# Moving the norms' sums to token partitions by small transfers, and making the last six tiles' sums in strips

## The chip, the cores and the metric

The kernel runs on one core of a Trainium2 chip. The core has TensorE (PE, the matmul engine, whose weight loads the profile lists apart as PEld), VectorE (DVE), ScalarE (ACT), GpSimd (POOL) and SyncE (SP), which here does nothing but issue transfers. Each engine runs its own instructions in order; semaphores make one wait for another. The metric is device time in microseconds (us) of one execution, the median of several.

## The reference

An encoder layer works on two sequences, a prompt of 256 tokens and a sample of 2,048, with a model width of 1,024, in float32:

```python
h = rms_norm(x, g_pre)
q, k, v, z_a, u_f, z_f = split(h @ w_in)            # six parts of width 512
y_a = neighbourhood_attention(q, k, v, rpb)         # 8 heads of 64, windows of 8 x 16 on a grid 64 wide
y_f = fourier_mix(u_f, w_fourier, b_fourier)        # 2-D FFT, real part, then a matrix and a bias
mixed = concat([rms_norm(y_a, g_na) * silu(z_a),
                rms_norm(y_f, g_f) * silu(z_f)])
out = mixed @ w_out
return x + rms_norm(out, g_post)
```

where `rms_norm(x, g) = x * rsqrt(mean(x * x) + 1e-6) * g` over the last axis. What matters here are the two norms in `mixed`: for each of the 2,304 tokens one factor from the mean square of 512 values of `y_a`, and one of `y_f`.

## The kernel before

The tokens are cut into 18 tiles of 128. Both halves of `mixed @ w_out` are made apart: for a tile, the product of the un-normed half with its part of `w_out` stands in PSUM with the tokens on the partitions, and its factor is applied on the way out, as one number for each partition. The factors stand in `invf` (Fourier half) and `inva` (attention half), tiles of 128 x 18, one column for each token tile. Values `y`, on the other hand, are kept with the channels on the partitions and the tokens along the free axis, and so are the sums of squares over the channels' blocks: `sqs` (Fourier) and `ysq` (attention), both 128 x 2,304. To get a factor, the 128 partitions of `sqs` or `ysq` have to be summed and the result, a row of tokens, be turned so that the tokens lie on partitions.

The part of the program around the change is written in a set order by hand: PE always, and from the last Fourier block on also ACT, DVE, POOL and SP run their instructions in the order in which the source issues them. It has two stages:

1. **The attention loop** (L1577), k from 2 to 36. There are 36 groups `G` (four pairs of heads, nine groups each). Step k makes the scores of group k (`scores`, L1184), its softmax (DVE L1206, ACT L1211, POOL L1218), and, for group k-1, the transposes of the weights in two halves (`transp`, L1508, into the PSUM tiles `ptb[0]` and `ptb[1]`, copied out as `pt` by ACT and DVE) and the product with the values (`pv`, L1524, into the PSUM tile of tag `c`, of which there is one). Between them stand 12 output matmuls of the Fourier half (`f_mm`, L1435, PSUM tile `po`), whose evacuation `f_evac` applies `invf`. `pv` also writes squares of `y_a` into `ysq` (ACT, and POOL from the second pair on). In steps 2 to 7 the last Fourier block's squares are made by ACT (L1634) and added into `sqs` by DVE (L1635), for the token ranges in the table `YSQ`; step 5 treats tokens 512 to 1,109, step 6 those to 1,707 and step 7 the rest. At the end of a step SP issues the loads of the next groups: `prep_v` (`v` and `za`, one step ahead) and `prep` (`ql`, three steps ahead). `split_q` on ACT takes `ql` up.
2. **The output loop** over the 18 tiles of the attention half (index j): `a_mm` (24 matmuls of 512 columns a tile), `a_evac` with `inva`, the last norm, and the residual.

The norms' factors are made like this. `norm_sums` multiplies the squares by a block of ones, 128 x 32, so that up to four token tiles land side by side as strips of 32 equal rows of `ptb[0]`; ACT copies them to the SBUF tile `nsb`, of which there is one. One step later `norm_turn` transposes `nsb` with PE into the PSUM tile `pn` (tag `c`), where each strip's first column holds the tokens of a tile on the partitions, and `rsq_ops` makes the factor: two ACT instructions (L1381 and L1382), one on DVE (L1383), and three more on DVE, which `run_later` issues somewhat later. The table `NT` tells in which step which tiles are turned: Fourier tiles in steps 4, 8, 10, 11, 12, attention tiles in 32, 34, 36, and the sums stand in the step before. The first two Fourier tiles are done by `f_norm`, and the last six attention tiles by `a_norm` at j=1: matmuls with a tile of `ysq` as weights and one column of ones, which put the tokens onto partitions at once.

The program has eight semaphores for transfers that SP uses in turn, and each transfer waits, before it is issued, until the eighth transfer before it has landed.

Of the kernel before, what the change touches and what calls it, by code (L numbers as in the profile page):

```python
# [10 lines left out]
F32 = mybir.dt.float32  # L11
# [157 lines left out]
def build(tc, A, O):  # L169
    nc = tc.nc  # L170
# [23 lines left out]
    ident = cst.tile([128, 128], F32, name="ident")  # L194
    ones = cst.tile([128, 1], F32, name="ones")
# [7 lines left out]
    invf = cst.tile([128, 18], F32, name="invf")  # L203
    inva = cst.tile([128, 18], F32, name="inva")
# [9 lines left out]
    ps = es.enter_context(tc.tile_pool(name="ps", bufs=3, space=PSUM))  # L214
# [503 lines left out]
    for c in range(3, 6):  # L718
# [7 lines left out]
        if c == 4:  # L726
# [33 lines left out]
    for b in range(16):  # L760
# [13 lines left out]
        if 2 <= b < 8:  # L774
            x, y = divmod(b, 2)
# [349 lines left out]
    def prep(g):  # L1125
        pr, ts = g["pr"], g["ts"]
        g["qh"] = jl.tile([128, 256], F32R, tag="qh", name="qh", bufs=4)
        g["ql"] = jl.tile([128, 256], F32R, tag="ql", name="ql", bufs=4)
        if g["R"] is None:
            q = qD[pr, :, ts].rearrange("p (b x) -> p b x", b=2)  # L1130
        else:
            sg, x = divmod(g["R"], 2)
            t0 = TP + 1024 * sg + 512 * g["hc"]
            q = qD[pr, :, t0:t0 + 512].rearrange("p (b x) -> p b x", b=2)[:, :, 128 * x:128 * x + 128]
        nc.sync.dma_start(g["ql"].bitcast(F32).rearrange("p (b x) -> p b x", b=2), q)
# [258 lines left out]
    def run_later():  # L1394
        while later:
            later.pop(0)()
# [79 lines left out]

    nsb = []

    def norm_sums(sq, ts):
        n = 32 * len(ts)  # L1480
        for x, t in enumerate(ts):
            nc.tensor.matmul(ptb[0][32 * x:32 * x + 32, :128], ones32, sq[:, t * 128:t * 128 + 128], start=True, stop=True)
        o = sm.tile([128, 128], F32, name="nsb", bufs=1)[:n]
        nc.scalar.copy(o, ptb[0][:n, :128])  # L1484
        nsb.append(o)

    def norm_turn(dst, ts):
        o = nsb.pop()
        n = 32 * len(ts)
        p = ps.tile([128, 128], F32, tag="c", name="pn", bufs=1)[:, :n]  # L1490
        nc.tensor.transpose(p, o, ident[:n, :n])
        ts = slice(ts[0], ts[-1] + 1)
        rsq_ops(dst[:, ts], p[:, ::32], ts.stop - ts.start, 1.0 / 512)

    def a_norm(ds):
        p = ps.tile([128, 128], F32, tag="c", name="pna", bufs=1)
        for j, d in enumerate(ds):
            nc.tensor.matmul(p[:, j:j + 1], ysq[:, d["t"] * 128:d["t"] * 128 + 128], ones, start=True, stop=True)
        n = len(ds)
        rsq_ops(inva[:, ds[0]["i"]:ds[0]["i"] + n], p[:, :n], n, 1.0 / 512)  # L1500

    def transp(g, b):
        ch = g["ch"][b]
# [13 lines left out]
    def pv(g):  # L1517
# [28 lines left out]
        if R is None or hc:  # L1546
# [1 line left out]

    WO = []

    NT = {4: range(2, 4), 8: range(4, 8), 10: range(8, 12), 11: range(12, 16), 12: range(16, 18),
          32: range(4), 34: range(4, 8), 36: range(8, 12)}

    YSQ = {2: [(Y2, 256, 512), (Y2, 512, 1024)], 3: [(Y, 256, 512), (Y2, 1024, 1664)], 4: [(Y2, 1664, 2304)],
           5: [(Y, 512, 1110)], 6: [(Y, 1110, 1708)], 7: [(Y, 1708, 2304)]}
# [17 lines left out]
    prep_v(G[2])  # L1573
    prep(G[4])
    ones32 = sm.tile([128, 32], F32, name="ones32", bufs=1)
    nc.vector.memset(ones32, 1.0)
    for k in range(2, len(G) + 1):  # L1577
        pr, i = divmod(k, 9)
        g, f = G[k] if k < len(G) else None, G[k - 1] if k else None
        if pr < 3:  # L1580
            if i == 3:
                KK[pr + 1] = load_k(pr + 1)
                for x in range(2):
                    fetch_k(KK[pr + 1], pr + 1, x)
            if i == 7:
                load_t(pr + 1, 0)
        if 0 < pr < 4 and i == 0:
            load_t(pr, 1)
        if pr < 4 and i == 3:
            load_t(pr, 2)  # L1590
        if k == 9:
            nc.sync.dma_start(gpb, pbc(A["gpost"]))
        if k == 23:
            wp = pt.enter_context(tc.tile_pool(name="wp", bufs=1, side="right"))
            WO.extend(wp.tile([128, 4, D], F32R, name="w0%d" % x) for x in range(2))
        if 24 <= k < 32:
            y = k - 24
            nc.sync.dma_start(WO[y % 2][:, y // 2].bitcast(F32), woD[0, y % 2, y // 2])
        x = k // 2 + 1
        if g:  # L1600
            scores(g)
            if 2 < k < 34 and k % 2 == 0:
                ys_mul(ftiles[x])
                if x + 1 < 18:
                    ys_load(ftiles[x + 1])
            bias_max(g, 0, 0)
            exps(g, 0, 0)
            bias_max(g, 0, 1)
            bias_max(g, 1, 0)
        if f:  # L1610
            transp(f, 0)
        if g:
            exps(g, 0, 1)
            bias_max(g, 1, 1)
            exps(g, 1, 0)
            f_mm(k, range(6))
            soft(g, 0)
            exps(g, 1, 1)
        else:
            a_mm(atiles[0], 0, range(6))  # L1620
        if k in NT:
            norm_turn(invf if k < 32 else inva, NT[k])
        if f:
            transp(f, 1)
        if g:
            if k + 1 < len(G):
                split_q(G[k + 1])
            soft(g, 1)
            if k == 2:
                ys_mul(ftiles[x])  # L1630
                ys_load(ftiles[x + 1])
        run_later()
        for v, x0, x1 in YSQ.get(k, []):
            nc.scalar.activation(v[:, x0:x1], v[:, x0:x1], AF.Square)  # L1634
            V.tensor_tensor(out=sqs[:, x0:x1], in0=sqs[:, x0:x1], in1=v[:, x0:x1], op=ALU.add)  # L1635
# [12 lines left out]
        if g:  # L1648
            f_evac(k)
        if f:  # L1650
            pv(f)
        if k + 1 in NT:
            norm_sums(sqs if k < 31 else ysq, NT[k + 1])
        if k == 12:
            pq_.close()
        if k + 1 < len(G):
            prep_v(G[k + 1])
        if k + 3 < len(G):
            prep(G[k + 3])
        if k == 28:  # L1660
            xk = [kp.tile([128, T], F32, tag=x, name="xk") for x in ("kh", "kl")]
        if 32 <= k < 36:
            x, d = k - 32, atiles[k - 32]
            d["xt"] = xk[x // 2][:, x % 2 * D:x % 2 * D + D]
            nc.sync.dma_start(d["xt"], A["xn"][d["t"] * 128:d["t"] * 128 + 128, :])
        if k == 32:
            ys_load(atiles[0])
        if k in (34, 35):
            ys_load(atiles[k - 33])
            of_load(atiles[k - 34])  # L1670
        if k == 36:
            ys_split(atiles[1])
# [65 lines left out]
    for j, d in enumerate(atiles):  # L1738
        if j + 3 < 18:
            ys_load(atiles[j + 3])  # L1740
        for x in range(2, 5) if j == 0 else (j + 4,):
            if x < 18:
                of_load(atiles[x])
                if x > 3:
                    xt_load(atiles[x])
        if j:
            a_mm(d, 0)
        if j == 1:
            a_norm(atiles[12:])
            run_later()  # L1750
        a_evac(d, 0)
        if j + 2 < 18:
            y_hi(atiles[j + 2])
        if j == 0:
            for n in range(2):
                nc.scalar.copy(ptb[n], gpb[:, n * 512:n * 512 + 512])
        if j == 17:
            last_tile(d, atiles[16])
            break
        if j:  # L1760
            factor(atiles[j - 1])
# [24 lines left out]
```

## Time and profile before

| | |
|---|---|
| Median of three runs | 970.5 us (969.4 to 972.34) |
| The profiled execution | 971.28 us, span of its instructions 969.5 us |
| Granted TensorE clock | 0.998 |
| PE, PEld | 959.5 us (99%), 800.4 us (83%) |
| DVE, ACT, POOL | 705.4 us (73%), 496.1 us (51%), 429.8 us (44%) |
| DMA | 279.37 MB in 146,382 packets, 288 GB/s in the mean |

A row of the timeline gives the start in us from the span's start, the duration in us, the engine, the source line, the operation with what it writes and reads, the shape and a count, since like neighbours are merged; in brackets stands how long the engine was idle before it, and what ended that. `SPq` rows are the issuing of transfers. For PE a shape such as 128*32 128x512 gives the rows and columns of the array that are used, and the moving operand. A row of a line's or tile's view gives the smallest, middle and largest duration in ns, then the first and last start. A row of the waits gives the total in us, how often, and the longest. Float32 matmuls with a full-precision operand appear as two instructions each (12 for the six of `a_norm`).

### The profile page before, as it was taken

Reading aid. Unit: us, or ns where it says so; the run is one execution under the profiler, and the core shown is the slowest. Engines: PE = TensorE matmul, PEld = TensorE weight load, DVE = VectorE, ACT = ScalarE, POOL = GpSimd, SP = SyncE. Lnnn points to the kernel's source line nnn. Section 1 sums busy time; section 2 is a strip of 40 time slices with the busy share of each in tenths; the row PEclk is TensorE's granted clock in tenths of the full one; section 3 lists DMA queues with packets and bytes.
Section 4 is the critical chain, followed back from the end, with each engine's and each line's share of the span. In section 5 each row is a group of like instructions: output and inputs, shape, how many; then the busy total and the mean of one; then the engine's idle time right before and its main releaser. Section 6 shows DMA issues by size and latency. Waiting matters only on the chain.

```text
span 969.5 us, 17019 instructions
## 1 busy us (share of the span) xinstructions
PE 959.5 (99%) x5745; PEld 800.4 (83%) x5745; DVE 705.4 (73%) x1306; ACT 496.1 (51%) x1078; POOL 429.8 (44%) x400
## 2 busy tenths in 40 slices
PE   9999999999999999999999999999999999999997
PEld 7889988888888888888888879878787888878886
DVE  6758988687886777797877345776765656649997
ACT  6835676423334533233344256677666676744443
POOL 3100002464751202665655033567677686524544
PEclk9999999999999999999999999999999999999999
DMA  9898796557748997599889898689877998979993
GB/s 334 309 380 316 256 346 245 199 198 261 294 186 353 343 413 258 198 364 344 308 297 333 294 324 328 190 272 297 264 227 249 278 302 283 293 253 324 344 338 133
DMA packets 146382, 279.37 MB, mean 288 GB/s; under 512 B 13730, under 2 KB 84216, under 8 KB 142904
## 3 DMA queue, kind: packets, MB, share of 16 engines
q1 hardware_dynamic: 145864, 277.89, 81.9%
q8 instruction: 46, 0.75, 0.3%
q10 hardware_dynamic: 432, 0.39, 0.1%
q14 instruction: 40, 0.33, 0.1%
HBM read 183.85 MB, written 101.52 MB: 294 GB/s over the span
## 4 chain that ended last, share of the span: by engine, by line
PE 94%; DMA 1%; DVE 1%; SPq 1%; issue 1%; ACT 1%; POOL 1%; DVEq 0%; ACTq 0%; POOLq 0%
PE po L1435 20%; PE mm L165 18%; PE mm L164 17%; PE mm L166 17%; PE pv L1524 5%; PE ptb L1508 5%; PE s L1184 4%; PE pab L1024 2%; DMA ut<-uN 1%; PE py L164 1%; PE py L166 1%; PE py L165 1%; SPq L367 1%; DMA gpre<-gpre 0%; PE ppq L1062 0%
## 5 line engine op out<-in xcount | busy, mean ns | idle before, releaser
L164 PE MATMUL mm<-xh,wa 128*128 128x512 f32 x448 | 174.4, 389 | 0.0
L165 PE MATMUL mm<-xl,wa 128*128 128x512 f32 x448 | 174.3, 389 | 0.0
L166 PE MATMUL mm<-xh,wa 128*128 128x512 f32 x448 | 174.3, 389 | 0.0
L536 POOL TENSOR_TENSOR ws<-wr 128x512 f32<-128x512 f32 x16 | 23.5, 1468 | 228.0 <-DMA wr<-wz 224.0
L1218 POOL TENSOR_SCALAR w<-w,m 128x465 f32<-128x465 f32 (+9 forms) x136 | 85.2, 639 | 44.1 <-DVE m L1215 34.1
L164 PEld LDWEIGHTS mm<-xh,wa 128*128 128x128 f32 x448 | 84.1, 188 | 17.7
L166 PEld LDWEIGHTS mm<-xh,wa 128*128 128x128 f32 x448 | 84.1, 188 | 17.4
L165 PEld LDWEIGHTS mm<-xl,wa 128*128 128x128 f32 x448 | 84.1, 188 | 17.4
L1435 PE MATMUL po<-wo,yh 128*128 128x512 f32 x272 | 90.5, 414 | 0.0
L551 DVE TENSOR_TENSOR wa<-wr,wa 128x512 fp32r<-128x512 f32 x60 | 69.3, 1162 | 27.2 <-ACT wa L550 27.0
L1435 PE MATMUL po<-w,yh 128*128 128x512 f32 x280 | 86.7, 391 | 0.0
L1211 ACT ACTIVATE w<-w,m 128x465 f32<-128x465 f32 (+9 forms) x136 | 78.3, 579 | 15.5 <-DVE m L1206 15.5
L1206 DVE CUSTOM_DVE_ANT_1 w<-s,tb 128x465 f32<-128x465 f32 (+8 forms) x124 | 61.2, 531 | 9.7 <-PE s L1184 9.2
L165 PE MATMUL mm<-vl,xh 128*128 128x512 f32 x168 | 65.6, 390 | 0.2 <-DVE vl L482 0.2
L166 PE MATMUL mm<-vh,xl 128*128 128x512 f32 x168 | 65.4, 389 | 0.0
L164 PE MATMUL mm<-vh,xh 128*128 128x512 f32 x168 | 65.4, 389 | 0.0
L589 POOL TENSOR_TENSOR mt<-mt,rmask 128x880 f32<-128x880 f32 (+2 forms) x24 | 50.8, 2131 | 32.1 <-DVE mt L585 19.8
L877 DVE TENSOR_TENSOR f<-u,mm 128x512 f32<-128x512 f32 x64 | 43.5, 680 | 29.2 <-PE mm L166 24.3
L1435 PEld LDWEIGHTS po<-w,yh 128*128 128x128 f32 x280 | 52.3, 188 | 10.9 <-issue 0.2
L1508 PE MATMUL ptb<-ident,w 128*120 128x128 f32 (+8 forms) x422 | 58.9, 277 | 1.0 <-ACT nsb L1484 0.9
L550 ACT CAST wa<-wr 128x512 fp32r<-128x512 f32 x60 | 36.4, 617 | 44.8 <-PE mm L166 19.3
L1508 PEld LDWEIGHTS ptb<-ident,w 128*120 128x120 f32 (+8 forms) x422 | 47.2, 140 | 13.8 <-issue 8.0
(263 smaller groups left out, 2391.8 us busy)
## 6 DMA issues: line engine op xcount, KB each, us to landing
wr<-wz SPq DMA_DIRECT2D x48, 512.0 KB
vl<-sD SPq DMA_DIRECT2D x20, 512.0 KB
xm<-xm SPq DMA_DIRECT2D x9, 1024.0 KB
oD<-ofs SPq DMA_DIRECT2D x18, 512.0 KB
of<-oD SPq DMA_DIRECT2D x18, 512.0 KB
yr<-yD SPq DMA_DIRECT2D x34, 256.0 KB
zD<-f SPq DMA_DIRECT2D x16, 512.0 KB
woD<-wo SPq DMA_DIRECT2D x16, 512.0 KB
```

The source lines that it names most:

```text
L164: nc.tensor.matmul(out, lh, rh, start=first, stop=False)
L165: nc.tensor.matmul(out, lh, rl, start=False, stop=False)
L166: nc.tensor.matmul(out, ll, rh, start=False, stop=last)
L551: nc.vector.tensor_tensor(out=o[:, 1], in0=src, in1=o[:, 0].bitcast(F32), op=ALU.subtract)
L589: nc.gpsimd.tensor_tensor(out=o, in0=i, in1=rmask[:, m0:m0 + n].unsqueeze(2).to_broadcast([128, n, 80]), op=ALU.add)
L877: nc.vector.tensor_tensor(out=dst(f, b), in0=src(uu[u]), in1=src(p), op=op)
L1206: nc.vector.tensor_tensor_reduce(out=rows(g["w"][b][:, h, :n], w), in0=rows(g["s"][2 * b + h][:, :nr * sw(w)], sw(w))[:, :, :w], in1=tv, s ...
L1211: nc.scalar.activation(w, w, AF.Exp, bias=m[:, h:h + 1], scale=-1.0, accum_out=m[:, 2 + h:3 + h])
L1218: nc.gpsimd.tensor_scalar(w, w, m[:, 4 + h:5 + h], 1.0, ALU.mult, ALU.mult)
L1435: nc.tensor.matmul(p, (d["l"] if x == 2 else d["h"])[:, c], w(n, int(x == 1), c), start=j == 0, stop=j == 11)
L1508: nc.tensor.transpose(ptb[h][:nk, j * 128:j * 128 + 128], g["w"][b][:, h, c0:c0 + nk], ident)
L1524: nc.tensor.matmul(p[hs, b], g["v"][:nk, v, hs], g["pt"][b][:nk, h, j * 128:j * 128 + 128], start=j == 0, stop=j == len(ch) - 1)
```

## The change

The turn by PE stays for the first group of Fourier tiles (step 4) only. For all others, `norm_move` sends, from `nsb`, the first row of each strip (128 floats on one partition) by a transfer of its own to one column of a new SBUF tile `ssum` (128 x 18, one float on each of 128 partitions). SP issues these at the end of the step in which the sums are made, behind `prep_v` and `prep`. `norm_root` then makes the factors from `ssum`, two and a half steps after the sums. So the sums of Fourier tiles 4 to 15 move to steps 5, 7, 9 (from 7, 9, 10); the attention tiles' sums stay in 31, 33, 35, and their roots come in 34, 36 and, for tiles 8 to 11, at j=1 of the output loop. The last six tiles use `norm_sums` too, with `ysq` as the moving operand: tiles 12 to 15 at j=1 and 16, 17 at j=2, into a PSUM tile of tag `c`, and one root for the six at j=5.

```diff
+    def norm_sums(sq, ts, p=None):
+        p = ptb[0] if p is None else p
         n = 32 * len(ts)
         for x, t in enumerate(ts):
+            nc.tensor.matmul(p[32 * x:32 * x + 32, :128], ones32, sq[:, t * 128:t * 128 + 128], start=True, stop=True)
+        o = sm.tile([128, 128], F32, tag="nsb", name="nsb", bufs=1)
+        nc.scalar.copy(o[:n], p[:n, :128])
+        nsb.append((ts, o))
...
+    def norm_move():
+        ts, o = nsb.pop()
+        for x, t in enumerate(ts):
+            nc.sync.dma_start(ssum[:, t:t + 1], o[32 * x:32 * x + 1, :])
+
+    def norm_root(dst, ts):
         ts = slice(ts[0], ts[-1] + 1)
-        rsq_ops(dst[:, ts], p[:, ::32], ts.stop - ts.start, 1.0 / 512)
-
-    def a_norm(ds):
-        p = ps.tile([128, 128], F32, tag="c", name="pna", bufs=1)
-        for j, d in enumerate(ds):
-            nc.tensor.matmul(p[:, j:j + 1], ysq[:, d["t"] * 128:d["t"] * 128 + 128], ones, start=True, stop=True)
...
+        rsq_ops(dst[:, ts], ssum[:, ts], ts.stop - ts.start, 1.0 / 512)
+
+    def a_norm(ts):
+        norm_sums(ysq, ts, ps.tile([128, 128], F32, tag="c", name="pna", bufs=1))
+        norm_move()
...
-    NT = {4: range(2, 4), 8: range(4, 8), 10: range(8, 12), 11: range(12, 16), 12: range(16, 18),
-          32: range(4), 34: range(4, 8), 36: range(8, 12)}
+    NS_ = {3: range(2, 4), 5: range(4, 8), 7: range(8, 12), 9: range(12, 16), 11: range(16, 18),
+           31: range(4), 33: range(4, 8), 35: range(8, 12)}
+    NR_ = {8: range(4, 8), 10: range(8, 12), 12: range(12, 16), 14: range(16, 18), 34: range(4), 36: range(4, 8)}
...
-        if k in NT:
-            norm_turn(invf if k < 32 else inva, NT[k])
+        if k == 4:
+            norm_turn()
+        if k in NR_:
+            norm_root(invf if k < 32 else inva, NR_[k])
...
-        if k + 1 in NT:
-            norm_sums(sqs if k < 31 else ysq, NT[k + 1])
+        if k in NS_:
+            norm_sums(sqs if k < 31 else ysq, NS_[k])
...
+        if nsb and k > 3:
+            norm_move()
...
         if j == 1:
-            a_norm(atiles[12:])
-            run_later()
+            norm_root(inva, range(8, 12))
+        if j in (1, 2):
+            a_norm(range(4 * j + 8, min(4 * j + 12, 18)))
+        if j == 5:
+            norm_root(inva, range(12, 18))
+        run_later()
```

More of the change, by code (lines that the diff above doesn't have):

```diff
@@ L1477, in build, with norm_turn @@
     nsb = []
-    def norm_sums(sq, ts):
+    def norm_sums(sq, ts, p=None):
+        p = ptb[0] if p is None else p
         n = 32 * len(ts)
         for x, t in enumerate(ts):
[L1482 to L1488, printed above, removed]
+            nc.tensor.matmul(p[32 * x:32 * x + 32, :128], ones32, sq[:, t * 128:t * 128 + 128], start=True, stop=True)
+        o = sm.tile([128, 128], F32, tag="nsb", name="nsb", bufs=1)
+        nc.scalar.copy(o[:n], p[:n, :128])
+        nsb.append((ts, o))
+    def norm_turn():
+        ts, o = nsb.pop()
         n = 32 * len(ts)
         p = ps.tile([128, 128], F32, tag="c", name="pn", bufs=1)[:, :n]
-        nc.tensor.transpose(p, o, ident[:n, :n])
-        ts = slice(ts[0], ts[-1] + 1)
-        rsq_ops(dst[:, ts], p[:, ::32], ts.stop - ts.start, 1.0 / 512)
-    def a_norm(ds):
-        p = ps.tile([128, 128], F32, tag="c", name="pna", bufs=1)
-        for j, d in enumerate(ds):
-            nc.tensor.matmul(p[:, j:j + 1], ysq[:, d["t"] * 128:d["t"] * 128 + 128], ones, start=True, stop=True)
-        n = len(ds)
-        rsq_ops(inva[:, ds[0]["i"]:ds[0]["i"] + n], p[:, :n], n, 1.0 / 512)
+        nc.tensor.transpose(p, o[:n], ident[:n, :n])
+        rsq_ops(invf[:, ts[0]:ts[-1] + 1], p[:, ::32], len(ts), 1.0 / 512)
+    def norm_move():
+        ts, o = nsb.pop()
+        for x, t in enumerate(ts):
+            nc.sync.dma_start(ssum[:, t:t + 1], o[32 * x:32 * x + 1, :])
+    def norm_root(dst, ts):
+        ts = slice(ts[0], ts[-1] + 1)
+        rsq_ops(dst[:, ts], ssum[:, ts], ts.stop - ts.start, 1.0 / 512)
+    def a_norm(ts):
+        norm_sums(ysq, ts, ps.tile([128, 128], F32, tag="c", name="pna", bufs=1))
+        norm_move()
     def transp(g, b):
@@ L1575, in build @@
     ones32 = sm.tile([128, 32], F32, name="ones32", bufs=1)
+    ssum = sm.tile([128, 18], F32, name="ssum", bufs=1)
     nc.vector.memset(ones32, 1.0)
```

## The prediction

> **What bounds the kernel now.** I read the page first (busy times, slices, the chain), then the tiles `pn` and `pna`, then the timeline around each place that the diff touches.
>
> ```profile
> PE 959.5 (99%) x5745; PEld 800.4 (83%) x5745; DVE 705.4 (73%) x1306; ACT 496.1 (51%) x1078; POOL 429.8 (44%) x400
> PE 94%; DMA 1%; DVE 1%; SPq 1%; issue 1%; ACT 1%; POOL 1%; DVEq 0%; ACTq 0%; POOLq 0%
> q1 hardware_dynamic: 145864, 277.89, 81.9%
> ```
>
> TensorE (PE) is busy for 959.5 of 969.5 us and holds 94% of the chain; the transfers take 81.9% of the DMA engines' time. So an edit counts by the PE time it takes away or adds, and by any new place at which PE stands still. A busy PE says little on how densely its matmuls follow one another, so I price PE work by the distance between the *starts* of neighbours, not by durations.
>
> **Transposes removed.** `norm_turn` goes from eight calls to one (k=4 stays), so seven transposes into `pn` leave PE. Six turn 128 rows, one (k=12) turns 64.
>
> ```profile
> L1491 PE MATMUL pn<-ident,nsb x8: 270/272/273, 634.4 to 861.4; 128*128 128x128 f32 x6, 64*128 64x64 f32 x2
> 861.15 0.39 PE L1435 MATMUL po<-w,yl 128*128 128x512 f32 x1
> 861.38 0.27 PE L1491 MATMUL pn<-ident,nsb 128*128 128x128 f32 x1
> 861.49 0.82 PE L1508 MATMUL ptb<-ident,w 128*96 128x128 f32 x6
> 691.55 0.40 PE L1435 MATMUL po<-wo,yl 128*128 128x512 f32 x1
> 691.88 0.27 PE L1491 MATMUL pn<-ident,nsb 64*128 64x64 f32 x1
> 692.08 0.86 PE L1508 MATMUL ptb<-ident,w 128*88 128x128 f32 x6
> ```
>
> One lasts 0.27 us, but the next starts 0.11 after it, and that is its price: 6 x 0.11 = 0.66. The 64-row one puts 0.53 between the `po` matmul and the next transpose, where 0.23 is usual (861.15 to 861.38): 0.30. Together **-0.96 us**.
>
> **The last six tiles.** `a_norm` had `ysq` as weights, 12 instructions; now `ones32` is the weight and tiles go side by side into four strips of columns, as `norm_sums` does: four tiles at j=1, two at j=2.
>
> ```profile
> 870.02 0.62 PE L1435 MATMUL po<-w,yh 128*128 128x512 f32 x2
> 870.71 1.39 PE L1498 MATMUL pna<-ones,ysq 128*128 128x1 f32 x12
> 871.96 0.72 PE L1435 MATMUL po<-w,yh 128*128 128x512 f32 x2
> 659.82 1.27 PE L1524 MATMUL pv<-pt,v 120*64 120x128 f32 x20
> 661.02 0.43 PE L1482 MATMUL ptb<-sqs,ones 128*32 128x128 f32 x8
> 661.37 0.44 PE L1184 MATMUL s<-kh,qh 64*128 64x384 f32 x2
> 634.02 0.40 PE L1435 MATMUL po<-wo,yl 128*128 128x512 f32 x1
> 634.35 0.27 PE L1491 MATMUL pn<-ident,nsb 64*128 64x64 f32 x1
> ```
>
> Removed: 870.71 to 871.96 is 1.25, and the two `po` behind it span 0.72 instead of 0.62, so 0.10 more: 1.35. Added: a block of four tiles takes 661.02 to 661.37 = 0.35. Going from `po` into a narrower shape the next start came 0.33 later instead of 0.23 (634.02 to 634.35): 0.10 in, and I take the 0.10 seen above out. That makes 0.55 a block, two blocks 1.10. No row shows a strip block between `po` matmuls: the ends are 0.35 a block (nothing for the switches) and 0.85 (0.30 more, what the 64-row turn cost in all), so removal and addition come to a gain of 0.65 at best and a loss of 0.35 at worst. I take **-0.25**, by the nearest rows. By the Trainium skill (TensorEngine Tiling (Array Packing), Key Properties) a change of tiling mode, not of the tile alone, drains the array. With no drain the two blocks would cost 0.70 and the gain would be 0.65; with it the 0.25 stands, and the rows at 634.02 and 634.35, a change of shape without strips, agree in kind.
>
> **Sums moved up.** They stood at k=3, 7, 9, 10, 11 and stand at 3, 5, 7, 9, 11: as many blocks, but that at k=5 is new and k=10 loses one. Four strips of k=5 read `sqs` columns 512 to 1024, and the last square for these is added by L1635 in the same step. Its rows, and the steps around it:
>
> ```profile
> 638.47 0.57 SPq L1135 DMA_DIRECT2D ql<-qD  x1
> 644.45 1.75 PE L1524 MATMUL pv<-pt,v 120*64 120x128 f32 x28
> 645.04 0.41 ACT L1163 CAST qh<-ql 128x256 fp32r<-128x256 f32 x1 [1.48 <-DMA ql<-qD]
> 645.35 0.70 ACT L1634 ACTIVATE Y<-Y 128x598 f32<-128x598 f32 x1
> 646.08 0.82 DVE L1635 TENSOR_TENSOR sqs<-sqs,Y 128x598 f32<-128x598 f32 x1 [2.27 <-ACT Y L1634]
> 646.14 0.19 PEld L1184 LDWEIGHTS s<-kh,qh 64*128 64x128 f32 x2 [0.17 <-ACT Y L1634]
> 647.42 0.41 DVE L1538 TENSOR_TENSOR y<-pv,za 128x256 f32<-128x256 f32 x1
> 647.50 0.87 PE L1508 MATMUL ptb<-ident,w 128*120 128x128 f32 x6
> 647.86 0.38 ACT L1540 ACTIVATE ysq<-pv 128x256 f32<-128x256 f32 x1
> 858.90 0.26 ACT L1484 COPY nsb<-ptb 128x128 f32<-128x128 f32 x1
> 859.30 0.85 PE L1508 MATMUL ptb<-ident,w 128*128 128x128 f32 x6 [0.89 <-ACT nsb L1484]
> ```
>
> ACT stood 1.48 us until `ql` had landed; its square and the addition on DVE are late with it. The addition ends at 646.90. A wait of PE on another engine ended 0.14 after that engine's work (859.16 to 859.30), so the sums could begin at 647.04. PE is done with `pv` and would begin them at 646.14. So PE, which had no wait here, gets one: **+0.90**. Bounds: nothing, if `ql` lands in time (without 1.48 the addition ends at 645.42); 2.4, if `ql` is late by 1.48 once more. I take 0.90, as all that is issued before k=5 is unchanged.
>
> Behind the sums the transposes of k=6 overwrite `ptb[0]` and wait for the copy `nsb`. `y` on DVE ends at 647.83, `ysq` on ACT at 648.24, the copy 0.26 later at 648.50, PE may go at 648.64. PE comes there at 647.04 + 0.35 + 1.36 (646.14 to 647.50) = 648.75. Hidden with 0.11 to spare; if that cover goes, what is lost is at most the 0.89 that k=36 pays now and will go on paying.
> The roots are as many as before, ten; one now falls at j=5, and ACT gets two more copies of 0.26 (ten for eight), all in the output stage.
>
> ```profile
> core 0: us, PE busy (x) PEld busy (x) DVE busy (x) ACT busy (x) POOL busy (x), PEclk, DMA share, GB/s
> 865.00:948.00 83.00, 83.00 (x375) 68.83 (x372) 76.17 (x151) 38.84 (x110) 36.04 (x29) 1.00 0.94 325
> ```
>
> There DVE has 6.8 us free of 83 and ACT 44, while PE has none: the root and the copies are hidden by PE's matmuls; uncovered, the copies alone would cost 0.52.
>
> **The transfers.** Thirty-two transfers of 128 floats (four groups of sums for f: 4, 4, 4, 2; three for a: 4 each; six at the end) pass through SP, each spread over 128 partitions.
>
> ```profile
> 651.42 0.43 SPq L1135 DMA_DIRECT2D ql<-qD  x1
> 656.99 0.32 SPq L1106 DMA_DIRECT2D tb<-tD  x1
> 660.94 0.32 SPq L1465 DMA_DIRECT2D oD<-ofs  x1
> SPq L1465 <- ACT ofs L1464: 32.1, 16, 5.4
> SPq L1547 <- DVE y L1538: 28.0, 15, 5.4
> 661.88 0.26 ACT L1484 COPY nsb<-ptb 128x128 f32<-128x128 f32 x1
> 662.50 0.31 PE L1508 MATMUL ptb<-ident,w 128*96 128x128 f32 x1
> 678.94 0.43 SPq L1135 DMA_DIRECT2D ql<-qD  x1
> 688.85 0.25 ACT L1484 COPY nsb<-ptb 64x128 f32<-64x128 f32 x1
> ```
>
> An issue takes 0.43 us, four 1.72, all of them 13.8 us of SP. What waits behind them are the loads of the next step. Cover: after 656.99 SP stands until 660.94 for a result of ACT, and such waits add up to 60.1 us over 31 times, 1.9 each, more than a group takes. In the program each transfer also waits on the eighth one before it, so a group holds four of eight places while it flies; loads have a step or more to spare but for `ql`, and a `ql` later by 1.7 us would hold ACT, not PE. On the DMA engines 32 x 128 = 4,096 small packets come to 145,864: at the mean packet of q1 (81.9% x 969.5 x 16 / 145,864 = 0.087 us) 0.7 us a transfer with eight packets an engine, surely less at 4 bytes. At k=35 SP now waits for the copy (859.16), and three loads behind slide by some 3 us; they serve the output stage. I set all this at 0, from -0.5 (DVE and ACT no longer wait for `pn` and `pna`) to +1.
>
> **The sum.** -0.96 - 0.25 + 0.90 = -0.3 us. The profiled execution took 971.28 us around its span of 969.5, 0.8 above the median of 970.5, which is the frame of the forecast: **970.2 us**, no change that could be measured: the three runs spread from 969.4 to 972.34, and 0.3% (2.9 us) is about what this kernel can tell from no change.
>
> **Rivals.**
> - *No wait at k=5.* `ql` lands earlier in other executions; then -0.96 - 0.25 = -1.2: 969.3. For it: it hangs on one transfer that took 6.5 us (638.47 to 645.04). Against: its queue is the same in both kernels up to there.
> - *The removed matmuls were not the limit.* If the gaps of 0.11 close without gain and the blocks cost their upper end (+0.35), they and the wait remain: 971.8. Against: neighbours' starts are even to 0.01.
> - *The copy is late at k=6 too.* +0.9 more: 971.1. The spare 0.11 speaks for it.
> - *Slower: the transfers land too late.* `nsb` has one buffer, so the copy at k=7 (661.88) must wait until the four transfers of k=5 have landed, and PE's transposes wait for the copy with 0.22 us of slack (662.50 - 662.14 - 0.14). These are issued behind `ql`, 651.85 to 653.6; likewise those of k=9, 679.4 to 681.1, against the copy at 688.85. That allows 8.3 and 7.8 us; the one flight that the rows show took 6.5, behind large loads. From about 8 us on every further us is lost at four copies (k=7, 9, 11, 33). At 10 us I get 1.5 and 2.0 for the two shown, some 7 in all: 977. The roots have 12 us and matter later. By the Trainium skill (DMA: Bandwidth & Descriptors, Rules for kernel authors) a last dimension that isn't contiguous becomes one descriptor for each element. That makes 128 pieces of each transfer, which speaks for this rival; no run here shows such a transfer.
>
> **How the numbers follow.** The sum as worked out 0.48, no wait at k=5 0.16, matmuls no limit 0.07, late copy 0.07, late landing 0.14, and 0.08 for a gain that I do not see. The first four lie within 2.9 us of 970.5 and hold 0.78; the spread of the runs takes 0.06 of that out, to both sides alike. A landing of 8 to 9 us (0.02) stays inside as well. So faster 0.11, same 0.74, slower 0.15. The range goes from 968.2 (no wait, and 1.1 of the runs' spread) to 973.6, where landing takes some 9 us.
>
> **What would show it.** Right: seven `pn` fewer, `po` to `ptb` 0.23 at k=8; a PE wait of about 0.9 on DVE `sqs` before the sums at k=5; two strip blocks of about 0.35 in the output stage; ACT's roots without a wait for a transfer; PE busy near 99%. Wrong: ACT waiting at the `nsb` copies or at L1381 on a DMA, PE idle before `ptb`, or loads of `v`, `za` or `ql` that arrive late behind the small transfers.

## The result, and the profile after

The changed kernel takes 974.61 us in the median (971.92 to 976.61) against 970.5 (969.4 to 972.34); the ratio is 1.0042, with a 95% interval of [1.0024, 1.006]. So it is some 4 us slower, and the forecast of 970.2 us (968.2 to 973.6), no change that could be measured, was wrong. The profiled execution took 976.29 us, 1.7 above the median.

The page of the changed kernel, engines, chain by engine, and the first DMA queue:

```profile
PE 961.4 (99%) x5738; PEld 799.5 (82%) x5738; DVE 708.0 (73%) x1306; ACT 496.9 (51%) x1080; POOL 428.6 (44%) x400
PE 93%; DMA 2%; DVE 1%; POOL 1%; SPq 1%; issue 1%; ACT 1%; DVEq 0%; POOLq 0%; ACTq 0%
q1 hardware_dynamic: 150472, 277.91, 82.1%
```

The bytes and the share of the DMA engines have hardly moved, but DMA has 2% of the chain where it had 1%. The waits of PE from 640 to 880 us say with what (line, what it waited for, us in total, times, longest). In the kernel before there was one group alone, the first line here; the others are those after the change:

```profile
PE ptb L1508 <- ACT nsb L1484: 0.9, 1, 0.9
PE ptb L1514 <- ACT nsb L1485: 1.2, 2, 0.9
PE pv L1530 <- DMA v<-vD: 1.2, 3, 0.5
PE s L1184 <- ACT qh L1163: 0.7, 2, 0.4
PE s L1184 <- POOL ql L1164: 0.2, 1, 0.2
```

PE now also waits for `v`, and for the halves of `q` that ACT and POOL make from `ql`. The places, in the timeline after the change, are steps 11 to 13:

```profile
687.61 0.44 PE L1530 MATMUL pv<-pt,v 101*64 101x128 f32 x4 [0.46 <-DMA v<-vD]
688.34 0.40 ACT L1163 CAST qh<-ql 128x256 fp32r<-128x256 f32 x1 [3.15 <-DMA ql<-qD]
688.80 0.44 PE L1184 MATMUL s<-kh,qh 64*128 64x360 f32 x2 [0.41 <-ACT qh L1163]
696.42 0.44 PE L1530 MATMUL pv<-pt,v 101*64 101x128 f32 x4 [0.49 <-DMA v<-vD]
697.89 0.40 ACT L1163 CAST qh<-ql 128x256 fp32r<-128x256 f32 x1 [3.02 <-DMA ql<-qD]
698.35 0.49 PE L1184 MATMUL s<-kh,qh 64*128 64x480 f32 x2 [0.34 <-ACT qh L1163]
```

Matched by their order, a matmul that started at 698.49 before starts at 703.03 now: 4.54 us later, while at 681.57 (now 680.98) it was still 0.59 ahead. All of the loss, and more, arises in these 17 us.

Why the loads are late stands in SP's rows, of which some are shown here. Before, then after (start, duration, what is issued):

```profile
664.28 0.43 SPq L1135 DMA_DIRECT2D ql<-qD  x1
664.76 0.47 SPq L1405 DMA_DIRECT2D yr<-yD  x1
667.88 0.41 SPq L1109 DMA_DIRECT2D tb<-tD  x1
674.25 0.32 SPq L1465 DMA_DIRECT2D oD<-ofs  x1
678.20 0.70 SPq L1159 DMA_DIRECT2D za<-zD  x1
685.50 0.43 SPq L1135 DMA_DIRECT2D ql<-qD  x1
```

```profile
651.08 2.48 SPq L1498 DMA_DIRECT2D ssum<-nsb  x4
664.73 0.43 SPq L1135 DMA_DIRECT2D ql<-qD  x1
666.24 2.79 SPq L1498 DMA_DIRECT2D ssum<-nsb  x4
669.08 0.59 SPq L1405 DMA_DIRECT2D yr<-yD  x1
672.31 0.41 SPq L1109 DMA_DIRECT2D tb<-tD  x1
674.12 0.32 SPq L1465 DMA_DIRECT2D oD<-ofs  x1
680.17 4.06 SPq L1159 DMA_DIRECT2D za<-zD  x1
684.27 0.44 SPq L1135 DMA_DIRECT2D ql<-qD  x1
685.12 3.23 SPq L1498 DMA_DIRECT2D ssum<-nsb  x4
693.70 0.43 SPq L1135 DMA_DIRECT2D ql<-qD  x1
```

At the `ql` of step 7 (664.73) SP was 0.45 us behind the kernel before; at the `yr` and the table `tb` (1,200 KB) that follow the small transfers of that step it is 4.3 us behind. SP itself makes this up while it waits for the next result `ofs`: the store `oD` goes out at 674.12, where it went at 674.25. But the table was issued 4.4 us late, and `za` of step 9, eight places behind it, must wait until it has landed; then it takes 4.06 us to issue, where it took 0.70. The `ql` behind it comes 5.3 us late (684.27 for 678.94), and behind the next four small transfers the last `ql` here, that of step 10, is issued 8.2 us later than before. Such long issues exist in the kernel before as well (3.92 us for the `za` at 634.50); what makes them long is not shown by any run. The waits are in SP's list from 655 to 700 us:

```profile
SPq L1159 <- DMA tb<-tD: 1.5, 1, 1.5
SPq L1498 <- DMA tb<-tD: 1.0, 1, 1.0
SPq L1498 <- DMA oD<-ofs: 1.0, 2, 0.5
```

The first small transfer of step 7 stands eight places behind the 880 KB table of that step (657.99), and waits until it has landed; the second waits 0.5 us for a store `oD` in the same way. So of the 3.9 us between the end of that `ql` and the `yr` at 669.08, some 1.5 are waits for landings, and most of the rest is the issue of the four.

### The profile page after: what moved, and what is told of

Read it like the earlier page. It is cut to its first block, busy times and chain, and to the rows that moved or that the text cites. A ratio compares the mean times of both kernels' runs of the same rounds, so it can differ in the third digit from the quotient of the medians.

```text
span 974.4 us, 17077 instructions
## 1 busy us (share of the span) xinstructions
PE 961.4 (99%) x5738; PEld 799.5 (82%) x5738; DVE 708.0 (73%) x1306; ACT 496.9 (51%) x1080; POOL 428.6 (44%) x400
## 3 DMA queue, kind: packets, MB, share of 16 engines
q1 hardware_dynamic: 150472, 277.91, 82.1%
## 4 chain that ended last, share of the span: by engine, by line
PE 93%; DMA 2%; DVE 1%; POOL 1%; SPq 1%; issue 1%; ACT 1%; DVEq 0%; POOLq 0%; ACTq 0%
PE po L1435 18%; PE mm L164 18%; PE mm L165 18%; PE mm L166 18%; PE pv L1530 5%; PE ptb L1514 5%; PE s L1184 4%; PE pab L1024 2%; DMA v<-vD 1%; PE py L164 1%; PE py L166 1%; PE py L165 1%; DMA gpre<-gpre 0%; ACT w L1211 0%; DMA ql<-qD 0%
## 5 line engine op out<-in xcount | busy, mean ns | idle before, releaser
L1518 DVE COPY pt<-ptb 120x384 f32<-120x384 f32 (+5 forms) x72 | 40.5, 563 | 29.8 <-PE ptb L1514 28.0
```

## The experiments

The theory (A): the small transfers hold SP, by their issue and by the landing of the eighth transfer before each, and in SP's set order the loads behind them are late, `v` and `ql` above all. The rival (B): the 4,096 pieces of 4 bytes load the DMA engines. A second rival (C): the sums, copies and roots that moved are what costs, not the transfers. All diffs are against the changed kernel where nothing else is said.

Two numbers are drawn from each trace. *Delay of SP*: from the start of the first score matmul of step 6 to the issue of the `ql` of step 10, less the same before (646.14 to 685.50, 39.36 us). *PE, steps 6 to 15*: from that matmul to the same late `pv` matmul of step 15 (717.99 before), less the same before; here the change saves four turns (0.63 by the forecast) and a block of sums that went to step 5 (0.35), so -0.98 is what an undisturbed kernel with the Fourier part of the change should show. The kernels in which these steps have neither small transfers nor moved sums (e4, e11, e13) read about -0.15 where nothing is due, which tells how finely the column can be read.

| Kernel | Ratio to before [95%] | Delay of SP, us | PE, steps 6 to 15, us |
|---|---|---|---|
| changed | 1.0042 [1.0024, 1.006] | 8.2 | +4.55 |
| small transfers through POOL (e1) | 1.006 [1.0041, 1.0079] | (PE itself late) | +4.92 |
| 32 floats each (e2) | 1.0029 [1.0011, 1.0047] | 5.2 | +0.77 |
| one of four (e3) | 0.9997 [0.9983, 1.0011] | 1.2 | -1.01 |
| Fourier part undone (e4) | 0.9995 [0.9983, 1.0007] | -0.2 | -0.15 |
| attention part undone (e5) | 1.0026 [1.0012, 1.0041] | 6.5 | +2.00 |
| before, with small transfers (e6) | 1.0025 [1.001, 1.0041] | 5.3 | +0.61 |
| `gpb` later (e7) | 1.0009 [0.9995, 1.0023] | 5.8 | +2.00 |
| two a step (e8) | 1.0052 [1.0036, 1.0069] | 0.9 | +1.36 |
| two a step, second tile (e9) | 1.001 [0.9997, 1.0022] | 2.2 | -0.74 |
| two transfers a group (e10) | 1.0009 [0.9998, 1.002] | 0.1 | -0.98 |
| before, with the strips (e11) | 1.0001 [0.9991, 1.001] | -0.2 | -0.16 |
| two a step, `gpb` later (e12) | 0.9997 [0.9982, 1.0012] | 0.5 | -1.00 |
| before, `gpb` later (e13) | 1.0004 [0.999, 1.0018] | -1.1 | -0.15 |
| two transfers, `gpb` later (e14) | 0.9995 [0.998, 1.0011] | -0.9 | -1.00 |

The traces are of one execution each, and executions spread: that of e2 was the fastest of its kernel (969.97 us, median 973.41), that of e7 3.4 us above its median. The two columns on the right belong together; the ratio is of all.

**The transfers on another queue (e1).**

```diff
-            nc.sync.dma_start(ssum[:, t:t + 1], o[32 * x:32 * x + 1, :])
+            nc.gpsimd.dma_start(ssum[:, t:t + 1], o[32 * x:32 * x + 1, :])
```

> The changed kernel, but the 32 small transfers are issued by GpSimd (POOL) instead of SP; on that queue they have eight places of their own. Theory A (SP's order: the four transfers of a group, each of which waits for the landing of the eighth transfer before it, push the loads of the next steps back by some 4 us at k=7 and up to 8 us at k=9 to 11, and PE then waits for v and ql): SP is as early as before at step 8 (yr issued at about 664.8), no PE wait on a DMA between 687 and 703, and the time is that of before less seven transposes and the strips, 969 to 970 us. Theory B (the 4,096 pieces of 4 bytes load the DMA engines and slow the other transfers, whoever issues them): as slow as the changed kernel, 974 to 975 us. Against A it could go if POOL is held by the issuing for long: PE would then wait at pt or sqa.

Measured: 976.92 us against 970.25, so the time that A gave is refuted. The trace shows why, and it is neither theory: from 640 us on PE waits for no `v` any more, and once (0.8) for the half of `q` that POOL makes from `ql`. But one wait of 3.0 us is new, at step 9, and its chain runs over a DVE operation on 128 x 4 numbers:

```profile
669.19 3.61 DVE L1388 SCALAR_TENSOR_TENSOR invf<-dt,dy 128x4 f32<-128x4 f32 x1
668.95 0.99 POOL L1218 TENSOR_SCALAR w<-w,m 128x288 f32<-128x288 f32 x2
669.91 1.52 POOL L1113 TENSOR_TENSOR tb<-cm,tb 128x640 f32<-128x640 f32 x1
671.40 1.39 POOL L1096 TENSOR_TENSOR kl<-kl,kh 128x576 fp32r<-128x576 f32 x1
672.91 0.75 DVE L1467 TENSOR_SCALAR ofs<-po,invf 128x512 f32<-128x512 f32 x1
673.72 0.72 PE L1435 MATMUL po<-wo,yh 128*128 128x512 f32 x2 [3.04 <-DVE ofs L1467]
```

The operation, which takes 0.16 us where nothing meets it, ends at 672.80, when POOL's row of work ends (672.79). POOL is late because it had issued four small transfers for 2.18 us. So the queue of SP was relieved as A says, and POOL's time was paid for it. For the contest of A and B this run decides little.

**Fewer pieces, or fewer transfers (e2, e3).**

```diff
-            nc.sync.dma_start(ssum[:, t:t + 1], o[32 * x:32 * x + 1, :])
+            nc.sync.dma_start(ssum[:32, t:t + 1], o[32 * x:32 * x + 1, :32])     # e2
...
-        for x, t in enumerate(ts):
+        for x, t in list(enumerate(ts))[:1]:                                    # e3
```

Both fill `ssum` with 1.0 beforehand and leave out most of the moved sums, so many tokens are scaled by a wrong factor.

> The changed kernel with transfers of 32 floats instead of 128: as many transfers and places, a quarter of the pieces (the factors of the other tokens are left out, so that part of the output is scaled wrongly). Theory A: as slow as the changed kernel, 974 to 975 us, since the count of transfers is what pushes SP back; the issue time could become a little shorter. Theory B: the loss falls to about a quarter, 970.5 to 971.5 us.

> The changed kernel with only the first transfer of each group, of 128 floats (the other tiles' sums are left out, their factors are wrong): a quarter of the transfers and of the pieces. Theory A: SP loses about 1 us a group instead of 4, which loads with a step to spare can bear: 969 to 971 us. Theory B: also 970 to 971.5. Only with the run of 32 floats beside it does it tell the two apart: A wants these two 4 us apart, B wants them equal. If both stay at 974 to 975, neither theory holds, and the cause is in the sums or the roots.

Measured: 973.41 and 970.43 us against 970.25. Both move a quarter of the pieces. With as many transfers the loss stays for the most part (1.0029 for 1.0042), with a quarter of the transfers it is gone. The two are 3 us apart where A wanted 4 and B none, though the intervals of their ratios touch at 1.0011. So A fits and B is not the main cause; that the pieces have some part in the loss is not excluded by these two runs.

**One part undone (e4, e5).**

```diff
-    NS_ = {3: range(2, 4), 5: range(4, 8), 7: range(8, 12), 9: range(12, 16), 11: range(16, 18),
+    NS_ = {3: range(2, 4), 7: range(4, 8), 9: range(8, 12), 10: range(12, 16), 11: range(16, 18),
...
-        if k == 4:
+        if k in (4, 8, 10, 11, 12):
             norm_turn()
...
-        if nsb and k > 3:
+        if nsb and k > 30:
```

This is e4; e5 has the Fourier part as changed, with turns at 32, 34, 36 and the old `a_norm`.

> The changed kernel with the Fourier tiles' part undone: sums at k=7, 9, 10, 11 and turns by PE at 8, 10, 11, 12 as before; the attention tiles keep the small transfers, and the last six tiles the strips. By the traces of before and after (start of the same matmuls): the Fourier part cost +4.54 us by 703, so without it the time is 970 to 971 us: three transposes less (-0.33), waits at k=31 and 32 (+0.7 to +0.9), strips (-0.5). If the time stays at 974, the loss in k=11 to 13 of the one trace isn't typical.

> The changed kernel with the attention tiles' part undone (turns by PE at 32, 34, 36 and the six-tile sums with ysq as weights, as before); the Fourier tiles keep the sums at 3, 5, 7, 9, 11 and the small transfers. Theory A puts the whole loss here: by 703 the changed kernel's matmuls start 4.5 us later than before's, so 974.5 to 975.5 us. If the Fourier part and the attention part only lose together, 970 to 971.

Measured: 970.15 us (before: 970.25) for e4, 973.73 (before: 971.68) for e5. The loss sits in the Fourier part. Its size came out below the expectation: 2 us above the kernel before, where 974.5 to 975.5 us were expected, though the intervals of e5 and of the changed kernel overlap. One thing in the expectation of e4 was wrong: it counted the late waits as part of what the change costs. They do come in its trace (PE loses 0.79 us from 830 to 850), but at matmuls that start up to 838.77, while the first small transfer of that part is issued at 839.47; and they come as well in the kernel before with nothing but the load of `gpb` moved (e13, below), which has no small transfer at all:

```profile
834.84 1.75 PE L1524 MATMUL pv<-pt,v 120*64 120x128 f32 x28 [0.36 <-DMA v<-vD]
836.11 0.41 ACT L1163 CAST qh<-ql 128x256 fp32r<-128x256 f32 x1 [2.28 <-DMA ql<-qD]
```

So steps 30 to 33, behind a load of `woD` (512 KB) in each step from 24 to 31, are a second place that is tight for transfers, and the profiled execution of before was one that came through without a wait.

**The transfers alone (e6).** Against the kernel before:

```diff
+    dmy = sm.tile([128, 4], F32, name="dmy", bufs=1)
...
             prep(G[k + 3])
+        if k in (5, 7, 9, 11):
+            for x in range(4 if k < 11 else 2):
+                nc.sync.dma_start(dmy[:, x:x + 1], ident[32 * x:32 * x + 1, :])
```

> The kernel before, unchanged but for small transfers of 128 floats from a constant tile into a scratch tile at the end of steps 5, 7, 9 (four each) and 11 (two), behind the loads of prep. No sum, copy, turn or root is moved. Theory A: the loads of the next steps are pushed back as in the changed kernel, and the four turns that the change saves here (0.6 us) stay: 974 to 976 us. Rival: the loss comes from the sums and roots that moved (the sums of k=9 beside the load of gpb, the roots that read SBUF): 970 to 971.

Measured: 972.81 us against 971.68, ratio 1.0025. The transfers cost by themselves, with no sum, copy or root moved, so C is refuted as the main cause. The size is less than expected (1.001 to 1.0041, so 1 to 4 us above the kernel before; 974 to 976 us were foreseen): here no transfer waits for the copy `nsb` on ACT, and SP's delay is 5.3 us where the changed kernel has 8.2. In its trace no wait of PE is long enough for the list; PE falls back by 0.6 us at step 15, where ACT waits for a late `ql` (it had no wait there before):

```profile
709.18 0.41 ACT L1163 CAST qh<-ql 128x256 fp32r<-128x256 f32 x1 [2.33 <-DMA ql<-qD]
```

**The big load beside them (e7, e13).**

```diff
-        if k == 9:
+        if k == 14:
             nc.sync.dma_start(gpb, pbc(A["gpost"]))
```

e7 is the changed kernel with this edit, e13 the kernel before with it.

> The changed kernel with the load of gpb (512 KB, issued at the start of step 9 behind a table of 1,200 KB) moved to step 14. Theory A: the small transfers alone push SP back by 4 us at k=7; that this becomes 8 at k=9 is due to the tables which SP then issues late and whose landing the next transfers wait for. Without gpb 1.8 us of queue (512 KB at 290 GB/s) fall away, and the loss falls to 2 to 3 us: 972 to 973. If the tables have no part in it, 974.6 as the changed kernel; if they are all of it, 970.

> The kernel before with nothing changed but the load of gpb, from step 9 to step 14. Theory A: before has slack in the queue at step 9, so nothing: ratio 0.9995 to 1.0005. If gpb is a burden whoever stands beside it, 0.997 to 0.998, the 3 us that its move gave the changed kernel.

Measured: 972.16 us for e7 (1.0009), 971.13 for e13 (1.0004 [0.999, 1.0018]). By the times, moving 512 KB out of step 9 takes most of the loss away where the small transfers are (a loss of 2 to 3 us was expected to stay, 0.5 is measured, 2.2 at the upper end of the interval), and does nothing that can be told where they are not. So `gpb` costs only beside the small transfers. It is not the whole of it: the trace of e7, of an execution 3.4 us above the median, still has the `za` of step 9 behind the late table (3.91 us of issue at 680.26), and PE gives 3.0 us away in steps 6 to 15 (+2.00 for -0.98).

**The four spread out (e8, e9).** Two transfers at the end of the step of the sums, two at the end of the next; e9 also gives the copies of steps 7, 11 and 33 a tile of their own.

```diff
+        x1 = x0 + 2 if part else len(ts)
+        if x1 < len(ts):
+            nsb.append((ts, o, x1))
...
+        if (sq is sqs and ts[0] in (8, 16)) or (sq is ysq and ts[0] == 4):     # e9 alone
+            o = sm.tile([128, 512], F32, tag="jk", name="nsb", bufs=1)[:, :128]
```

> The changed kernel with each group's four transfers in two halves: two at the end of the step of the sums, two at the end of the next. As many transfers and pieces in all, but never more than two of the eight places at a time, and SP is held for about half as long at one place. Theory A: loads that have a step to spare bear half the delay, 970 to 972 us. If the total of transfers counts, wherever they stand, 974 to 975.

> The same halves of two transfers a step as in the run before, but the groups of steps 7, 11 and 33 use another tile (an idle one of 128 x 512) for their copied sums, so no copy waits for the second half of the group before to land. In the run with one tile PE lost 4.1 us at the transposes that wait for nsb, and nothing on v. If that single tile was what cost there and halves cure the delay of the loads (theory A), the time is that of before or up to 1 us less: ratio 0.999 to 1.001. If the total of transfers costs wherever it stands, v and ql are late again: 1.003 to 1.005.

Measured: 976.15 us for e8 (1.0052), no better than the change itself, and 971.4 against 970.97 for e9. e8 missed, by a wait that I had put among the forecast's rivals and forgotten in designing it. With the second half a step later, the one tile `nsb` isn't free in time:

```profile
687.26 1.77 SPq L1502 DMA_DIRECT2D ssum<-nsb  x2
691.38 0.26 ACT L1485 COPY nsb<-ptb 64x128 f32<-64x128 f32 x1 [2.79 <-DMA ssum<-nsb]
691.69 0.87 PE L1518 MATMUL ptb<-ident,w 128*120 128x128 f32 x6 [2.30 <-ACT nsb L1485]
```

With another tile this is gone, and PE's waits from 640 to 880 us in the trace of e9 are those of before: the 0.9 us of the transposes behind `nsb`, once, and nothing else.

**Half the transfers (e10).** One transfer takes the first rows of a group to DRAM, one brings them back turned a step later.

```diff
-            nc.sync.dma_start(ssum[:, t:t + 1], o[32 * x:32 * x + 1, :])
+        nc.sync.dma_start(scr[a:b], o[:32 * len(ts):32, :])
...
+            nc.sync.dma_start(ssum[:, a:b], scr[a:b].rearrange("t p -> p t"))   # at the end of the next step
```

> The changed kernel with two transfers a group instead of four: one takes the first rows of all strips (4 x 128 floats) to DRAM at the end of the step of the sums, one brings them back turned, 128 x 4, at the end of the next step. As many pieces of 4 bytes in all (512 in one transfer), half the transfers, one a step, and the work is complete. Theory A (count and order): like the run with one transfer of four, from k=6 on 1 to 1.6 us shorter than before, ratio 0.998 to 0.9995. If the pieces count (512 in one transfer held up as four of 128): v and ql late, 1.002 to 1.005.

Measured: 971.6 us against 970.97, 1.0009 [0.9998, 1.002]; the expected gain did not show in the time. In the trace steps 6 to 15 are as expected (SP's delay 0.1 us, PE -0.98), with all the pieces of 4 bytes there, which is a stronger stroke against B than e2. Then, from 813 to 837 us, with no small transfer since step 12 (the next is issued at 837.65), PE loses 3.0 us, 1.3 of it in one wait for `v` at 834.39: the second tight place again.

**The strips alone (e11).** The kernel before with the new sums of the last six tiles, their transfers and one root:

```diff
-            a_norm(atiles[12:])
             run_later()
+        if j in (1, 2):
+            a_norm(range(4 * j + 8, min(4 * j + 12, 18)))
+        if j == 5:
+            rsq_ops(inva[:, 12:18], ssum[:, 12:18], 6, 1.0 / 512)
+            run_later()
```

> The kernel before with the last six tiles alone changed: strips at j=1 and 2, six small transfers, one root at j=5; all turns by PE stay. In the changed kernel's trace the first block of strips brought the matmuls behind it 0.93 us ahead and the second cost 0.43, 0.5 in all where 0.25 was forecast: ratio 0.9995 (0.9985 to 1.0005 with the spread of the runs). The trace is to show the same two steps, -0.9 and +0.4, and nothing else.

Measured: 970.93 us against 970.97, 1.0001 [0.9991, 1.001]: no difference that can be told. PE loses 1.9 us between 717 and 850 in that execution (the second tight place) and gains 0.27 from 850 to the end.

**Both remedies (e12, e14).** e12 is e9 with `gpb` in step 14, e14 is e10 with it.

> Two small transfers a step with two tiles for the copied sums, and the load of gpb moved from step 9 to step 14. By theory A neither v nor ql is late between k=9 and k=13, in hardly any execution, and the turns (some -1.2 us from k=6 to 36 in the trace of the version without the move) and the strips (-0.4) remain: ratio 0.9985 to 0.9995. If the place that is tight for transfers at k=29 to 31, where no small transfer is near, takes the gain back in the common execution, 1.000.

> Two transfers a group by way of DRAM, and the load of gpb moved to step 14. As for the halves: 0.9985 to 0.9995 by theory A, 1.000 if the place at k=29 to 31 takes it back.

Measured: 970.37 and 970.73 us against 971.28, ratios 0.9997 [0.9982, 1.0012] and 0.9995 [0.998, 1.0011]. PE gains 1.00 us in steps 6 to 15 in both traces, and 1.06 and 0.89 to the end. That the change so mended beats the kernel before is thus seen in the traces, but not in the times; neither version can be called faster.

## Why the prediction was wrong, point by point

- **Transposes removed, -0.96: right.** Where a turn fell away at step 8, `po` and the first transpose now stand 0.23 apart; the shifts at the seven places in the trace of e12 are 0.10 to 0.12 six times and 0.30 once, at step 12.

```profile
664.20 0.39 PE L1435 MATMUL po<-wo,yl 128*128 128x512 f32 x1
664.43 0.82 PE L1514 MATMUL ptb<-ident,w 128*128 128x128 f32 x6
```

- **The last six tiles, -0.25: right.** In the changed kernel the block of four tiles costs 0.09 on the way in (0.32 for 0.23), 0.36 itself and 0.11 on the way out (0.73 for 0.62): 0.56 where 0.55 was forecast.

```profile
875.60 0.39 PE L1435 MATMUL po<-w,yl 128*128 128x512 f32 x1
875.92 0.43 PE L1483 MATMUL pna<-ysq,ones 128*32 128x128 f32 x8
876.28 0.73 PE L1435 MATMUL po<-w,yh 128*128 128x512 f32 x2
```

The expectation of e11 had 0.5, because I had read the shifts too coarsely; from 850 us to the end the traces with strips show -0.27 (e11), and -0.35 to -0.38 where a turn falls away as well.

- **The wait at k=5, +0.90: the mechanism is right, the size was too large.** It hangs on when `ql` lands, as the rival said. In the changed kernel ACT waited 0.77 for it (before: 1.48), the squares were in at 645.71, and PE went on without a stop; in the traces of e1 and e7 it waited 0.5.

```profile
643.86 0.41 ACT L1163 CAST qh<-ql 128x256 fp32r<-128x256 f32 x1 [0.77 <-DMA ql<-qD]
644.90 0.81 DVE L1645 TENSOR_TENSOR sqs<-sqs,Y 128x598 f32<-128x598 f32 x1 [1.56 <-ACT Y L1644]
645.77 0.43 PE L1483 MATMUL ptb<-sqs,ones 128*32 128x128 f32 x8
```

- **The copy and the roots behind other work: right.** The copy at k=6 held nobody up.
- **The transfers, 0 (from -0.5 to +1): this term failed.** The change came out 4.1 us slower although the turns and strips save some 1 us in the traces of e12 and e14, so by estimate the term is about 5 us; in the profiled execution it is 5.5 (+4.55 where -0.98 was due). Three steps in it were wrong.
  - *The issue.* The four of the first group took 2.48 us, not 1.72. The `yr` behind them, at step 6, came 1.7 us late, but only because SP had been 0.9 us ahead at the `ql` before them (650.55 against 651.42); that the number agrees is luck.
  - *The cover.* It was taken as a mean, "1.9 each" of SP's waits, over the whole loop. The wait that could hide the four of step 7 is there, but behind the loads of step 8 and the table, not in front of them: SP makes its delay up only before the `oD` at 674.12. And the first of the four had to wait itself, eight places behind a table of 880 KB; nothing was worked out for those places beyond saying that a group holds four of eight.
  - *What stays late.* SP was back on time, the loads were not: the table issued 4.4 us late held the `za` of step 9, and the four of step 9 came on top. The `yr` of steps 6, 8 and 10 are late by 1.7, 4.3 and 9.0 us, until with 8.2 at the `ql` the "step or more to spare" of the loads is used up. Steps 12 and 13 begin at 688.34 and 695.73 before, so a step is some 7 us.

  The table of the experiments shows that turn: with a delay of up to 2.2 us PE keeps its gain but for 0.2 us (e8 aside, where `nsb` was late), at 5.2 to 6.5 it gives 0.6 to 3.0 us away, at 8.2 it gives 5.5.
- **"A `ql` later by 1.7 us would hold ACT, not PE"** is right for 1.7 us; it was later by 8, and it held both.
- **The rival on the other side, transfers that land too late for the copies: not what happened**, though it exists. The copies waited for a landing only in the output stage in the changed kernel (4.1 us at 886.8, with PE's work going on), and the same wait cost PE 2.3 us at one place when e8 sent half of a group a step later. The descriptors of 4 bytes, which by the Trainium skill (DMA: Bandwidth & Descriptors, Rules for kernel authors) a last dimension that isn't contiguous makes, were not the trouble. The profile bears the page out in kind: its first queue has 4,608 packets more than before (150,472 for 145,864), 144 for each transfer of 128 elements. But in e10 steps 6 to 15 keep their gain with as many elements to move, and in e2 most of the loss stays with a quarter of them.
- **What would show it wrong** named loads of `v` and `ql` that arrive late behind the small transfers. That is what the trace has; the forecast listed the sign and gave it no chance of its own.

What remains unsettled: how much of SP's delay over the whole stretch is issue and how much waiting for places was not separated by a run, since the number of places was not changed in any; the rows tell it for step 7 alone. The loss of the transfers alone (e6) is about 2.4 us, and that of the Fourier part alone (e5) 2.5 us, less than that of the whole change (4 us). The intervals overlap, and whether the rest is the wait for `nsb` in front of each group is argued, not shown.

## What to carry to other kernels

A queue that is issued in a set order has no mean slack: for each transfer that is added, look at the step where it stands, at which transfer it must wait for (the eighth before it, here a table of 880 KB), and at whether the queue's next idle time comes before the loads behind it or after them. A queue that is back on time says nothing of its loads: here a table issued 4.4 us late held up the eighth transfer behind it after SP had caught up. In these runs the small transfers cost by their number and their place in the order rather than by their bytes or pieces, and loads with about one step to spare, some 7 us, bore a delay of 2 us and lost time at 5 to 8. Where executions spread by 3 us, the same stretch of PE in two traces tells a microsecond that the times don't, but a wait must be seen in more than one trace before it is laid to the change.

## What the runs showed of the hardware

- **A stall can cost twice.** After the waits of steps 11 to 13 the matmuls of the changed kernel run slower without any wait: from 698.35 to 703.03 they fall back by another 1.9 us. The stretches of 4 us show the granted clock, and a shorter one between them the part in which it was low (columns: stretch, its length, busy time and number of instructions of PE, PEld, DVE, ACT, POOL, then clock, DMA share, GB/s):

```profile
696.00:700.00 4.00, 2.87 (x26) 1.97 (x28) 0.87 (x3) 0.79 (x2) 1.62 (x3) 0.94 0.81 237
699.55:702.96 3.41, 3.41 (x17) 2.82 (x14) 2.60 (x10) 2.35 (x7) 1.52 (x3) 0.50 0.72 206
700.00:704.00 4.00, 4.00 (x19) 3.17 (x18) 2.43 (x10) 3.14 (x9) 1.79 (x4) 0.63 0.79 259
```

  From 696 to 700 PE was idle for 1.13 us, in pieces of 0.5 at most, and then the clock was 0.50 for 3.41 us, which alone is 1.7 us of work. In e1, after one wait of 3.0 us, it fell to a mean of 0.69 for the stretch 676 to 680; in e8 a wait of 2.3 us left it at 1.00. What decides between these cases is not shown. Of the seven executions of the changed kernel the three longest (976.21 to 976.61 us) were granted 0.996 to 0.997 in the mean, the three shortest (971.92 to 973.99) 0.999. By the Trainium skill (TensorE: Matmul & The Clock Gate, What's actually happening) the clock falls after an idle window of about 3.4 us. Here it fell with no idle time of that length.

- **A tiny DVE operation can stand for the length of several POOL operations** (e1: 3.61 us for 128 x 4 numbers). The Trainium skill (SBUF — State Buffer, SBUF: two separate sides) says that a DVE operation with two inputs in SBUF and a GpSimd operation that reads SBUF exclude one another for a whole instruction. The trace agrees, and shows more: the DVE operation, begun at 669.19, ended with the last operation of POOL's unbroken row (672.80 and 672.79), not with the first.
